# A two-layer diffusion backbone on one core: the recurrence issued in a written order, and the second layer's modulation moved to the first feed-forward

## The chip, the cores and the metric

The kernel runs on one core of a Trainium2 chip. A core has a matrix engine (PE, whose weight loads are listed as PEld), a vector engine (DVE), a scalar engine (ACT) and GpSimd (POOL), each with its own queue that it works off in order, and DMA queues issued from SyncE (SP) and from POOL. The metric is the device time of one execution in microseconds. A difference under 0.3%, some 4.8 us, can't be told from no change by a measurement of this kernel.

## What is computed

Two layers over 256 latent tokens and 256 context tokens of width 1024, all in float32. Each layer is: half-step SwiGLU, token mixing, half-step SwiGLU, each with shift, scale and gate from a conditioning vector. Layer 0 mixes with a bidirectional RWKV-7 recurrence (12 heads of 64, in 6 pairs) and a Fourier mix; layer 1 (latent tokens alone) with a convolution and pooling.

```python
m_lat = split(silu(c) @ ada_w[i] + ada_b[i], 9)          # 9 x 1024 modulation values, layers 0 and 1
h = h + 0.5 * m[2] * swiglu(modulate(h, g, m[0], m[1]), w_gu, w_down)
# layer 0, for both directions d, first the context, then the latent tokens:
w  = exp(-0.6065 * sigmoid(w0[d] + tanh(wd) @ w_up[d]))
a  = sigmoid(a0[d] + ad @ a_up[d]);  kd = k * (1 + (a - 1) * k_a);  b = kk * a
S  = S * w - (S @ kk) b^T + v kd^T ;  y = S @ r           # per token
o  = (groupnorm(y[0] + y[1]) + bonus) * g
```

## The kernel before

**Stages.** The first feed-forward (both streams, 512 columns) fills 46 to 405 us of the trace; then come the input projection of the mixer (to about 546 us), the recurrence (546 to 865 us) with the output projection at its end, two feed-forwards of the latent stream, the convolution mixer and the last feed-forward. All weight matmuls of the feed-forwards are split into three products of rounded parts: `weight` (L190, L191) casts each 512 KB weight tile on ACT and takes the remainder `wlo` on DVE, and PE runs 24 matmuls on it.

**Modulation.** Layer 0's modulation from the third of its nine vectors on is made in the first feed-forward by `ada_job`: a 1 MB DMA on POOL's queue brings 256 rows of the transposed matrix, and DVE multiplies each 128x1024 half with silu(c) and sums along the row (`adaj`, L281), one instruction per 128 outputs and stream, 80 in all. `ffn(..., jobs=2)` runs two steps of these jobs before each weight pair. Layer 1's whole modulation is made in the recurrence by `ada_wide`: 18 blocks, each with 4 DMAs of 512 KB, 8 matmuls (L260, 512 columns each), a copy, 4 transposes (L268) and a small reduce (L269).

**Recurrence.** The tokens are handled in chunks of 64, in three groups of two head pairs. For a group, `features` (twice, one per pair j) builds decays, keys and queries for both directions; `inverse` inverts the 32x32 triangular blocks of all chunks by an elimination of 30 steps of two DVE instructions (L666, L668), between a transpose Y (L657) and two transposes (L673, L678), and then multiplies blocks together (L687, L698) into F. `chain` then goes through 8 steps, one per chunk (4 of context, 4 of latents): PE makes RH from the state XV and the masked products AG (L784), ACT copies RH (L787), PE applies F (L793), ACT and DVE copy UV (L795, L796), PE updates the state with BK (L804), and DVE adds it to the decayed state Xs of POOL (L776, L811). `prep` of the next step makes the pair products pg (L743, L746), AG's upper half (L750), AG's lower half (L755), RR, rs and BK. `rwkv_out` (twice a group) is the output of one pair: group norm, bonus and gate.

**Order.** Outside the recurrence and after the first feed-forward's start, instructions are ordered by a scheduler that takes each engine's ready instruction of highest priority, and priority follows the order in which the program is written. In the recurrence the program alternates: a piece of chain, then `PR[0] = 6` pieces of side work (features and inverse of the next group, then the outputs of the group before), then 4 to 5 pieces of `ada_wide`, whose matmuls stand at a lower priority.

Of the kernel before, what the change touches and what calls it, by code (L numbers as in the profile page):

```python
# [13 lines left out]
P = 128  # L14
D = 1024
# [64 lines left out]
def lay_out(a):  # L80
# [20 lines left out]
    d["adat"] = w[0].T.reshape(9 * KT // 2, 2, P, D)[KT:].transpose(0, 2, 1, 3)  # L101
    d["ada1"] = w[1].reshape(4, 2, P, 18, 512).transpose(3, 0, 2, 1, 4)
# [31 lines left out]
class Net:  # L134
# [113 lines left out]
    def ada_wide(self, b, pool):  # L248

        nc = self.nc  # L250
        ps = self.bank("ada")
        for q in range(4):
            w = self.wp.tile([P, KT, P], F32, tag="wraw", name=self.nm("wraw"), bufs=4)
            w = w.rearrange("p k c -> p (k c)").rearrange("p (k n) -> p k n", k=2)
            nc.sync.dma_start(w, self.ins["ada1"][b, q])
            for i in range(2):
                k = 2 * q + i
                g = k % 4
                with self.tc.high_priority(-200):
                    nc.tensor.matmul(ps[32 * g:32 * g + 32, :], lhsT=self.cs[:, k, :], rhs=w[:, i, :],  # L260
                                     start=k < 4, stop=k >= 4, tile_position=(0, 32 * g), skip_group_check=True)
                if i:
                    yield
        sb = self.mp.tile([P, 512], F32, tag="adas", name=self.nm("adas"), bufs=1)
        nc.scalar.copy(sb, ps)
        pt = self.bank("ada")
        for i in range(4):
            nc.tensor.transpose(pt[:, i * P:(i + 1) * P], sb[:, i * P:(i + 1) * P], self.ident)  # L268
        nc.vector.tensor_reduce(out=self.mod[1, 0][:, 4 * b:4 * b + 4], in_=pt.rearrange("p (b g v) -> p b v g", b=4, g=4)[:, :, 0, :],  # L269
                                axis=AX.X, op=ALU.add)  # L270
        yield

    def ada_job(self, blk, vecs):
# [269 lines left out]
    def features(self, G, j, wa, kz, vz, rz):  # L543
        nc, mp, ins = self.nc, self.mp, self.ins
        c = lambda t: t[:, j:j + 1]
        up = mp.tile([P, 2, P], F32, tag="up", name=self.nm("up"), bufs=1)
# [16 lines left out]
        yield  # L563
# [802 lines left out]
```

## Time and profile before

| | |
|---|---|
| device time, median of 3 runs | 1596.66 us (1593.55 to 1597.36) |
| profiled execution: device time, span of the trace | 1593.66 us, 1592.0 us |
| PE busy in the span, mean granted clock | 1488.8 us (94%), 0.963 |
| DVE, ACT, POOL busy | 1082.7, 675.4, 202.3 us |
| chain that ended last, share of the span | PE 80%, DVE 13% |

Times in the trace are microseconds from the span's start. A window gives each engine's busy time in a stretch, and the share of full speed that PE's clock was granted there (1.00 is 2.4 GHz, 0.50 would be 1.2 GHz throughout).

### The profile page before, as it was taken

What the parts mean: (1) busy time and instruction counts of PE and PEld (TensorE: products, weight loads), DVE (VectorE), ACT (ScalarE), POOL (GpSimd) and SP (SyncE); (2) the same over time, 40 slices, a digit from 0 to 9 for tenths busy, and PEclk for the clock granted to TensorE, in tenths of its full rate; (3) what the DMA queues carried; (4) which work ended last, traced back from release to release, by engine and by line L of the source; (5) the groups of instructions that cost most, each with busy time, mean ns of one, the idle gap of its engine ahead of it and who ended that gap; (6) DMA issues with size and microseconds to landing.
All of it is one profiled execution on the core that took longest, in us unless ns stands there. A gap on an engine that the chain in (4) does not pass through costs nothing.

```text
span 1592.0 us, 29925 instructions
## 1 busy us (share of the span) xinstructions
PE 1488.8 (94%) x12102; PEld 1279.8 (80%) x12102; DVE 1082.7 (68%) x1994; ACT 675.4 (42%) x1101; POOL 202.3 (13%) x293
## 2 busy tenths in 40 slices
PE   5999999999989979899998999999999986899997
PEld 3788888888877755455686999999999874899997
DVE  4799963334689699577266777657775399767753
ACT  3422222223454462542444555445554365445542
POOL 0000100000131151321211000000000075200000
PEclk9999999999999889999799999999999988899999
DMA  9676953232322025455432555655556432345562
GB/s 373 236 238 235 335 200 103 93 92 82 125 84 84 28 102 203 169 197 194 150 108 69 171 181 180 179 190 173 186 176 178 137 106 92 121 161 184 183 181 88
DMA packets 68810, 253.40 MB, mean 159 GB/s; under 512 B 8032, under 2 KB 10864, under 8 KB 63936
## 3 DMA queue, kind: packets, MB, share of 16 engines
q1 hardware_dynamic: 64080, 219.46, 42.0%
q0 software_dynamic: 4592, 32.03, 5.7%
q8 instruction: 95, 1.56, 0.4%
q14 instruction: 43, 0.35, 0.1%
HBM read 249.36 MB, written 2.10 MB: 158 GB/s over the span
## 4 chain that ended last, share of the span: by engine, by line
PE 80%; DVE 13%; ACT 2%; issue 2%; POOL 1%; DMA 1%; SPq 0%; POOLq 0%; DVEq 0%; ACTq 0%
PE gu L195 13%; PE gu L196 13%; PE gu L197 13%; PE down L195 7%; PE down L196 7%; PE down L197 7%; PE ada L260 3%; PE gu L970 1%; PE gu L1055 1%; DVE wlo L191 1%; DVE oo L1028 1%; DVE ocv L1028 1%; PE pg L746 1%; PE down L804 1%; PE misc L631 1%
## 5 line engine op out<-in xcount | busy, mean ns | idle before, releaser
L190 ACT CAST whi<-wraw 128x1024 fp32r<-128x1024 f32 (+1 forms) x298 | 304.6, 1026 | 524.1 <-PE gu L196 227.2
L191 DVE TENSOR_TENSOR wlo<-wraw,whi 128x1024 fp32r<-128x1024 f32 (+1 forms) x298 | 356.3, 1198 | 151.9 <-ACT whi L190 144.9
L195 PE MATMUL gu<-yh,whi 128*128 128x258 f32 (+1 forms) x1408 | 438.3, 312 | 6.2 <-ACT yh L375 4.3
L196 PE MATMUL gu<-yl,whi 128*128 128x258 f32 (+1 forms) x1408 | 437.7, 311 | 0.1
L197 PE MATMUL gu<-yh,wlo 128*128 128x258 f32 (+1 forms) x1408 | 436.8, 310 | 0.0
L195 PEld LDWEIGHTS gu<-yh,whi 128*128 128x128 f32 x1408 | 265.8, 189 | 24.1 <-ACT yh L375 5.7
L196 PEld LDWEIGHTS gu<-yl,whi 128*128 128x128 f32 x1408 | 267.2, 190 | 15.1 <-DVE yl L377 1.0
L197 PEld LDWEIGHTS gu<-yh,wlo 128*128 128x128 f32 x1408 | 267.3, 190 | 14.9 <-DVE wlo L191 0.8
L196 PE MATMUL down<-hl,whi 128*128 128x256 f32 (+1 forms) x704 | 217.3, 309 | 0.0
L195 PE MATMUL down<-hh,whi 128*128 128x256 f32 (+1 forms) x704 | 217.3, 309 | 0.0
L197 PE MATMUL down<-hh,wlo 128*128 128x256 f32 (+1 forms) x704 | 217.3, 309 | 0.0
L196 PEld LDWEIGHTS down<-hl,whi 128*128 128x128 f32 x704 | 134.4, 191 | 7.4
L195 PEld LDWEIGHTS down<-hh,whi 128*128 128x128 f32 x704 | 134.4, 191 | 7.4
L197 PEld LDWEIGHTS down<-hh,wlo 128*128 128x128 f32 x704 | 134.4, 191 | 7.4
L350 POOL TENSOR_TENSOR rs<-ms,mhalf 128x2 f32<-128x2 f32 (+1 forms) x9 | 10.9, 1208 | 821.4 <-DVE ms L347 821.4
L281 DVE SCALAR_TENSOR_TENSOR adaj<-adaw,cb 128x1024 f32<-128x1024 f32 x80 | 97.7, 1221 | 4.9 <-DMA adaw<-in_adat_dram 3.6
L260 PE MATMUL ada<-wraw,ccs 128*32 128x512 f32 x288 | 71.5, 625 | 0.7 <-DVE mod L269 0.7
L384 DVE SCALAR_TENSOR_TENSOR hlat<-down,mc,hlat 128x256 f32<-128x256 f32 x46 | 22.2, 483 | 63.0 <-PE down L197 63.0
L438 DVE COPY wb<-gu 128x1 f32<-128x1 f32 x132 | 20.2, 153 | 46.6 <-PE gu L197 46.6
L360 ACT CAST hh<-hd 128x256 fp32r<-128x256 f32 (+1 forms) x88 | 40.4, 461 | 25.0 <-DVE hd L433 14.2
L970 PE MATMUL gu<-yo,wraw 128*128 128x256 f32 x192 | 45.4, 396 | 1.9 <-ACT yo L375 1.9
L1012 POOL TENSOR_TENSOR opart<-opart,opr 128x256 f32<-128x256 f32 x54 | 44.9, 832 | 5.0 <-ACT opr L1010 1.2
(341 smaller groups left out, 2311.9 us busy)
## 6 DMA issues: line engine op xcount, KB each, us to landing
wraw<-in_gu_dram SPq DMA_DIRECT2D x176, 512.0 KB, 4.0
wraw<-in_ada_dram SPq DMA_DIRECT2D x72, 512.0 KB, 4.3
adaw<-in_adat_dram POOLq DMA_DIRECT2D x28, 1024.0 KB, 5.6
wraw<-in_down_dram SPq DMA_DIRECT2D x64, 448.0 KB, 3.3
wraw<-in_down_dram SPq DMA_DIRECT2D x32, 512.0 KB, 3.5
wraw<-in_win_dram SPq DMA_DIRECT2D x22, 512.0 KB, 3.8
wraw<-in_owin_dram SPq DMA_DIRECT2D x14, 512.0 KB, 3.6
ada<-in_ada_dram SPq DMA_DIRECT2D x4, 1024.0 KB, 16.8
```

The lines of the kernel that those rows point to most:

```text
L190: nc.scalar.copy(hi[:, :k, :], raw[:, :k, :])
L191: (eng or nc.vector).tensor_tensor(out=lo[:, :k, :], in0=raw[:, :k, :], in1=hi[:, :k, :].bitcast(F32), op=ALU.subtract)
L195: mm(ps, lhsT=wh, rhs=xh, start=start, stop=False, **k)
L196: mm(ps, lhsT=wh, rhs=xl, start=False, stop=False, **k)
L197: mm(ps, lhsT=wl, rhs=xh, start=False, stop=stop, **k)
L260: nc.tensor.matmul(ps[32 * g:32 * g + 32, :], lhsT=self.cs[:, k, :], rhs=w[:, i, :], start=k < 4, stop=k >= 4, tile_position=(0, 32 * g), ...
L281: nc.vector.scalar_tensor_tensor(out=junk, in0=w[:, i, :], scalar=1.0, in1=self.cb[v], op0=ALU.mult, op1=ALU.mult, accum_out=self.mod[0, v ...
L360: self.nc.scalar.copy(hi, x)
L384: nc.vector.scalar_tensor_tensor(out=h[v][:, k, :], in0=ps[:, n * T:n * T + T], scalar=gate[v][:, k:k + 1], in1=h[v][:, k, :], op0=ALU.mul ...
L970: nc.tensor.matmul(ps[:, :n], lhsT=w[:, k, :], rhs=y[:, k, :], start=k == 0, stop=k == KT - 1)
L1012: nc.gpsimd.tensor_tensor(out=part, in0=prev, in1=pr, op=ALU.add)
L1028: nc.vector.scalar_tensor_tensor(out=c, in0=u[:, w:w + T], scalar=cw[:, j, w:w + 1], in1=c, op0=ALU.mult, op1=ALU.add)
```

## The change

Three things are changed. `ada_wide` is gone, and 36 more `ada_job`s for layer 1 are appended to the list of the first feed-forward, which now takes three steps of it at each call. The recurrence is written inside a block in which PE, DVE, ACT and POOL keep the program's order: `chain` yields three times a step (after RH, after UV, at the step's end), and after each the class `Beside` lets the side work go on by 2.4, 2.6 or 1.7 us (by group) of costs that are written at the side work's yields. And some instructions change engine: AG's lower half, one half of ar, ac and the `f` of the decay from DVE to POOL; rs from DVE to ACT; the small copies pc and ps from POOL to ACT.

```diff
-    def ada_wide(self, b, pool):
...
-    def ada_job(self, blk, vecs):
+    def ada_job(self, l, blk, vecs):
...
-        nc.gpsimd.dma_start(w, self.ins["adat"][blk // 2 - KT])
+        nc.gpsimd.dma_start(w, self.ins["adat"][l * 9 * KT // 2 + blk // 2 - KT])
...
-                                               op1=ALU.mult, accum_out=self.mod[0, v][:, blk + i:blk + i + 1])
+                                               op1=ALU.mult, accum_out=self.mod[l, v][:, blk + i:blk + i + 1])
...
+            nc.gpsimd.tensor_scalar(out=f[:, :, 1:], in0=c8(th), scalar1=1.0, scalar2=1.0, op0=ALU.add, op1=ALU.mult)
...
-            nc.gpsimd.tensor_copy(G["pc"][:, x, :], em[:, :, CW])
+            nc.scalar.copy(G["pc"][:, x, :], em[:, :, CW])
...
-            nc.vector.tensor_tensor(out=G["ac"][:, x], in0=kr[:, 1], in1=em[:, NCH:, 0:CW], op=ALU.mult)
-            nc.vector.tensor_tensor(out=G["ar"][:, x, :, 1, :], in0=ch(rev(rz))[:, 0], in1=em[:, 0:NCH, 1:], op=ALU.mult)
+            nc.gpsimd.tensor_tensor(out=G["ac"][:, x], in0=kr[:, 1], in1=em[:, NCH:, 0:CW], op=ALU.mult)
+            nc.gpsimd.tensor_tensor(out=G["ar"][:, x, :, 1, :], in0=ch(rev(rz))[:, 0], in1=em[:, 0:NCH, 1:], op=ALU.mult)
...
-                nc.vector.tensor_tensor(out=AG[lo, hd], in0=G["ac"][r, :, c, :] if s else G["ar"][r, :, c, 0, :], in1=pc,
...
+                nc.gpsimd.tensor_tensor(out=AG[lo, hd], in0=G["ac"][r, :, c, :] if s else G["ar"][r, :, c, 0, :], in1=pc,
...
+                nc.scalar.copy(rs[lo], G["ar"][up, :, c, 1, :])
...
+class Beside:
+
+
+    def __init__(self):
+        self.gens, self.left = [], 0.0
+
+    def run(self, us):
+        self.left = min(self.left + us, us)
+        while self.gens and self.left > 0:
+            r = next(self.gens[0], self)
+            if r is self:
+                self.gens.pop(0)
+            else:
+                self.left -= 1.0 if r is None else r
+
+    def rest(self):
+        drive(self.gens, 1000)
...
+                    net.jobs += [net.ada_job(1, k, (0,)) for k in range(0, 9 * KT, 2)]
...
-                    net.ffn(0, h, yh, yl, gate, acc, fp, 2, start)
+                    net.ffn(0, h, yh, yl, gate, acc, fp, 3, start)
...
-            wide = [net.ada_wide(b, lp) for b in range(18)]
             outs = []
+            order = tc.manual_schedule(engines={mybir.EngineType.PE, mybir.EngineType.DVE, mybir.EngineType.Activation,
+                                                mybir.EngineType.Pool})
+            order.__enter__()
...
-                while next(it, it) is not it:
-                    drive(side, PR[0])
-                    drive(wide, PR[1 + g])
-                drive(side, 1000)
+                for _ in it:
+                    side.run((2.4, 2.6, 1.7)[g])
                 outs = [net.rwkv_out(*y, gs) for y in G[g]["y"]]
+                if g < 2:
+                    it = net.chain(G[g + 1], lp)
+                    next(it)
+                side.rest()
+            order.__exit__(None, None, None)
```

The outputs of group 0 join the list of group 1's stage behind its features and inverse, and what the slices don't reach is issued by `rest`, after the next chain's first preparation.

How PE's order moves is seen in chain 0, in one of its later steps. Before, between the matmuls that make RH (L784) and those that apply F (L793), stand matmuls and transposes of `ada_wide` (L260, L268):

```order
L784 MATMUL down_5632<-XV_5284,AG_5546 64x64
L260 MATMUL ada_5241<-wraw_5492,ccs 32x512
L260 MATMUL ada_5241<-wraw_5496,ccs 32x512 x2
L746 MATMUL pg_5681<-ar_3317,bk_3313 128x128 x2
L268 MATMUL ada_5502<-cst,adas_5500 128x128 x4
L732 MATMUL mx_5667<-cst,z_3301 128x128
L732 MATMUL mx_5667<-cst,vr_5669 128x128
L784 MATMUL down_5632<-XV_5284,AG_5546 64x64 x7
L732 MATMUL mx_5667<-cst,z_3481 128x128
L732 MATMUL mx_5667<-cst,vr_5673 128x128
L746 MATMUL pg_5681<-ar_3317,bk_3314 128x128 x2
L793 MATMUL down_5643<-RH_5641,A_3319 64x64 x8
L746 MATMUL pg_5681<-ar_3317,bk_3315 128x128 x2
L746 MATMUL pg_5681<-ar_3317,bk_3316 128x128 x2
```

After, at the like step, RH is L822 and F is L833, and BK's transposes (L749), the pair products (L764) and the state update (L845) follow as written:

```order
L822 MATMUL down_5536<-XV_5187,AG_5423 64x64 x8
L749 MATMUL mx_5550<-cst,bk_3529 128x128
L749 MATMUL mx_5550<-cst,bk_3530 128x128
L749 MATMUL mx_5550<-cst,bk_3531 128x128
L749 MATMUL mx_5550<-cst,bk_3532 128x128
L833 MATMUL down_5569<-RH_5545,A_3535 64x64 x8
L764 MATMUL pg_5580<-ar_3533,bk_3529 128x128 x2
L764 MATMUL pg_5580<-ar_3533,bk_3530 128x128 x2
L764 MATMUL pg_5580<-ar_3533,bk_3531 128x128 x2
L764 MATMUL pg_5580<-ar_3533,bk_3532 128x128 x2
L845 MATMUL down_5596<-UV_5188,BK_5431 64x64 x8
```

The matmuls on `wraw` are gone from between the chain's products, and RH's eight stand in one piece.

On DVE, in the elimination of the same group, before: chain instructions (UV L796, AG L750 and L755, XV L811, RR L759) alternate one by one with elimination instructions:

```order
L666 TENSOR_TENSOR sub_5172<-Y_5151,Z_5152 128x150
L668 TENSOR_TENSOR Z_5152<-Z_5152,sub_5172 128x25x6
L666 TENSOR_TENSOR sub_5175<-Y_5151,Z_5152 128x168
L796 TENSOR_SCALAR UV_5285<-down_5526 64x4x64
L668 TENSOR_TENSOR Z_5152<-Z_5152,sub_5175 128x24x7
L750 TENSOR_TENSOR AG_5546<-pg_5547,cst 64x512
L666 TENSOR_TENSOR sub_5178<-Y_5151,Z_5152 128x184
L755 TENSOR_TENSOR AG_5680<-ar_3317,pc_3320 64x256
L668 TENSOR_TENSOR Z_5152<-Z_5152,sub_5178 128x23x8
L811 TENSOR_TENSOR XV_5284<-down_5537,Xs_5513 64x4x64
L666 TENSOR_TENSOR sub_5181<-Y_5151,Z_5152 128x198
L759 TENSOR_TENSOR RR_5559<-pg_5547,cst 128x512
```

After (elimination L657 and L659, UV L836, AG's upper half L768), eight elimination instructions stand together ahead of UV, and AG's lower half is not on DVE:

```order
L657 TENSOR_TENSOR sub_5560<-Y_5407,Z_5408 128x210
L659 TENSOR_TENSOR Z_5408<-Z_5408,sub_5560 128x21x10
L657 TENSOR_TENSOR sub_5563<-Y_5407,Z_5408 128x220
L659 TENSOR_TENSOR Z_5408<-Z_5408,sub_5563 128x20x11
L657 TENSOR_TENSOR sub_5566<-Y_5407,Z_5408 128x228
L659 TENSOR_TENSOR Z_5408<-Z_5408,sub_5566 128x19x12
L836 TENSOR_SCALAR UV_5188<-down_5569 64x4x64
L768 TENSOR_TENSOR AG_5547<-pg_5580,cst 64x512
L657 TENSOR_TENSOR sub_5590<-Y_5407,Z_5408 128x234
L659 TENSOR_TENSOR Z_5408<-Z_5408,sub_5590 128x18x13
L657 TENSOR_TENSOR sub_5593<-Y_5407,Z_5408 128x238
L659 TENSOR_TENSOR Z_5408<-Z_5408,sub_5593 128x17x14
```

What moved is the elimination, from single instructions in gaps to pieces of eight between the chain's.

On DVE in the first feed-forward, some 36 weight tiles into it, before: the last row sums are done, and the rows are remainders (`wlo`) and the gate's products (hd, hl):

```order
L433 TENSOR_TENSOR hd_1630<-sg_1629,gu_1604 128x512
L191 TENSOR_TENSOR wlo_1790<-wraw_1791,whi_1789 128x1024
L361 TENSOR_TENSOR hl_1338<-hd_1630,hh_1337 128x512
L191 TENSOR_TENSOR wlo_1821<-wraw_1822,whi_1820 128x1024
L433 TENSOR_TENSOR hd_1704<-sg_1703,gu_1678 128x512
L191 TENSOR_TENSOR wlo_1871<-wraw_1872,whi_1870 128x896
L361 TENSOR_TENSOR hl_1338<-hd_1704,hh_1337 128x512
```

After, at a later weight tile (about the 60th of 68), row sums (L255, `adaj`) still stand three to a remainder:

```order
L190 TENSOR_TENSOR wlo_2718<-wraw_2719,whi_2717 128x1024
L335 TENSOR_TENSOR hl_2246<-hd_2550,hh_2245 128x512
L255 SCALAR_TENSOR_TENSOR adaj_2969,mod_77<-adaw_2967,cb 128x1024
L271 SCALAR_TENSOR_TENSOR mc_2442_13965<-mc_2442_13965,smallc 128x8
L255 SCALAR_TENSOR_TENSOR adaj_2971,mod_77<-adaw_2967,cb 128x1024
L255 SCALAR_TENSOR_TENSOR adaj_2975,mod_77<-adaw_2973,cb 128x1024
L190 TENSOR_TENSOR wlo_2749<-wraw_2750,whi_2748 128x1024
L255 SCALAR_TENSOR_TENSOR adaj_3013,mod_77<-adaw_2973,cb 128x1024
```

## Rows read from the trace of the kernel before

**Rows 1.** The page's first part: busy time, share of the span, instructions.

```profile
PE 1488.8 (94%) x12102; PEld 1279.8 (80%) x12102; DVE 1082.7 (68%) x1994; ACT 675.4 (42%) x1101; POOL 202.3 (13%) x293
```

**Rows 2.** Windows: stretch, length, busy PE, PEld, DVE, ACT, POOL (count); clock, DMA share, GB/s.

```profile
546.50:591.80 45.30, 36.55 (x580) 24.98 (x579) 37.89 (x65) 28.98 (x53) 22.64 (x34) 0.89 0.24 86
591.80:639.50 47.70, 45.30 (x580) 27.39 (x580) 44.44 (x115) 15.29 (x37) 7.92 (x11) 1.00 0.53 188
639.50:647.00 7.50, 7.18 (x273) 5.36 (x271) 2.02 (x6) 7.17 (x11) 1.89 (x2) 1.00 0.07 25
647.00:699.50 52.50, 47.38 (x577) 25.25 (x577) 34.50 (x61) 23.79 (x44) 21.68 (x30) 0.90 0.52 178
699.50:754.10 54.60, 50.53 (x572) 27.55 (x570) 43.37 (x112) 16.51 (x37) 7.83 (x12) 1.00 0.57 206
754.10:763.40 9.30, 9.24 (x265) 8.50 (x266) 0.43 (x3) 6.72 (x12) 1.87 (x4) 0.53 0.52 195
763.40:865.00 101.60, 93.83 (x931) 68.81 (x929) 55.69 (x119) 38.75 (x78) 20.20 (x22) 0.91 0.29 95
```

**Rows 3.** Windows of line L260 alone, over the recurrence; the sum.

```profile
sum 319.00, PE 71.50 PEld 10.56; mean PE 23.83 PEld 3.52
```

**Rows 4.** The chain of waits by line, 546 to 865 us.

```profile
by line: PE ada L260 15.2%; PE pg L746 5.4%; PE down L804 5.1%; PE misc L631 4.1%; issue 3.9%; PE down L784 3.8%; PE down L793 3.6%; DVE ff L591 3.3%; PE ada L268 2.8%; PE mx L765 2.7%; PE mx L829 2.3%; PE mx L823 2.2%; DVE AG L750 1.7%; PE
```

**Rows 5.** Groups of lines on DVE, 593 to 636 us (count; busy, mean ns; idle before).

```profile
L668 DVE TENSOR_TENSOR Z<-Z,sub 128x30 f32<-128x30 f32 (+14 forms) x30 | 10.9, 365 | 0.5
L666 DVE TENSOR_TENSOR sub<-Y,Z 128x30 f32<-128x30 f32 (+14 forms) x30 | 10.8, 359 | 0.5
L750 DVE TENSOR_TENSOR AG<-pg,cst 64x512 f32<-64x512 f32 x6 | 4.2, 695 | 0.4 <-PE pg L743 0.2
L755 DVE TENSOR_TENSOR AG<-ar,pc 64x256 f32<-64x256 f32 x6 | 3.4, 572 | 0.1
L811 DVE TENSOR_TENSOR XV<-down,Xs 64x256 f32<-64x256 f32 x8 | 3.4, 420 | 0.6 <-PE down L804 0.4
L796 DVE TENSOR_SCALAR UV<-down 64x256 f32<-64x256 f32 x5 | 2.1, 425 | 0.3 <-ACT UV L795 0.2
L673 DVE STREAM_TRANSPOSE A<-Z 128x1024 f32<-128x1024 f32 x1 | 2.0, 1995 | 0.0
```

**Rows 6.** Timeline of ACT: start, length, two successive copies of RH.

```profile
844.46 0.41 ACT L787 COPY RH<-down 128x256 f32<-128x256 f32 x1
851.08 0.37 ACT L787 COPY RH<-down 128x256 f32<-128x256 f32 x1 [5.04 <-PE down L784]
```

**Rows 7.** The page's costliest groups: the row sums of the first feed-forward.

```profile
L281 DVE SCALAR_TENSOR_TENSOR adaj<-adaw,cb 128x1024 f32<-128x1024 f32 x80 | 97.7, 1221 | 4.9 <-DMA adaw<-in_adat_dram 3.6
```

**Rows 8.** Windows of the first feed-forward.

```profile
160.00:200.00 40.00, 40.00 (x176) 32.64 (x175) 37.25 (x61) 9.83 (x12) 5.51 (x11) 1.00 0.93 337
220.00:400.00 180.00, 180.00 (x810) 147.97 (x809) 68.32 (x96) 48.52 (x67) 0.00 (x0) 1.00 0.30 95
```

**Rows 9.** Timelines of POOL and DVE around 599 us.

```profile
599.19 1.05 POOL L776 TENSOR_TENSOR Xs<-XV,pcs 64x512 f32<-64x512 f32 x1 [2.83 <-DVE XV L811]
599.29 1.05 DVE L668 TENSOR_TENSOR Z<-Z,sub 128x84 f32<-128x84 f32 x1
```

**Rows 10.** Timeline of DVE: first and last DVE work of one output (j).

```profile
763.56 0.42 DVE L849 SCALAR_TENSOR_TENSOR f<-misc,yy 128x256 f32<-128x256 f32 x1 [8.99 <-PE misc L847]
773.22 0.42 DVE L873 TENSOR_TENSOR z<-f,misc 128x256 f32<-128x256 f32 x1 [0.90 <-POOL f L870]
```

**Rows 11.** Windows of 20 us: one in the recurrence, one in the odd mixer.

```profile
760.00:780.00 20.00, 18.65 (x190) 11.56 (x184) 5.24 (x15) 8.64 (x17) 3.00 (x3) 0.67 0.32 116
1320.00:1340.00 20.00, 8.22 (x32) 6.41 (x31) 20.00 (x39) 10.51 (x24) 9.16 (x12) 0.79 0.18 60
```

**Rows 12.** Timeline of PE: a group of 16 in a slow stretch, one in a fast.

```profile
763.88 1.12 PE L784 MATMUL down<-XV,AG 64*64 64x64 f32 x16
851.51 0.68 PE L793 MATMUL down<-RH,A 64*64 64x64 f32 x16 [0.52 <-ACT RH L787]
```

More of the change, by code (lines that the diff above doesn't have):

```diff
@@ L558, in features @@
             nc.tensor.matmul(pt[:, 2 * i:2 * i + 2], lhsT=sq[:, P * i:P * i + P], rhs=self.hsel, start=True, stop=True)
+        for u, hi, lo in halves:
+            nc.vector.tensor_tensor(out=u[lo], in0=up[hi], in1=u[hi].bitcast(F32), op=ALU.subtract)
         mx = mp.tile([P, 4, 2], F32, tag="mx", name=self.nm("mx"), bufs=2)
@@ new lines, in values @@
+        def values(step):
+            s, c, _ = at(step)
+            ps = self.bank("ada")
+            for x in range(4):
+                v = G["v"][x][:, s, :]
+                if x % 2:
+                    vr = t([P, P], "vr", 2)
+                    nc.gpsimd.tensor_copy(vr, v[:, ::-1][:, c * CW:c * CW + P])
+                else:
+                    vr = v[:, c * CW:c * CW + P]
+                nc.tensor.transpose(ps[:, x * P:x * P + P], vr, self.ident)
+            for q in range(2):
+                V[step + q] = [t([P, 4, 2, CW], tag, 3) for tag in ("XV", "UV")]
+                for w in V[step + q]:
+                    nc.scalar.copy(w[up], xhi(ps)[CW * q:CW * q + CW])
@@ new lines, in keys @@
+        def keys(step, S):
+            s, c, ch = at(step)
+            S["XV"], S["UV"] = V.pop(step)
+            AG = S["AG"] = t([P, 2, 4, CW], "AG", 2)
+            for hd in range(2 if step else 0):
+                r = slice(CW * hd, CW * hd + CW)
+                pc = G["pc"][r, :, at(step - 1)[2]].unsqueeze(2).to_broadcast([CW, 4, CW])
+                nc.gpsimd.tensor_tensor(out=AG[lo, hd], in0=G["ac"][r, :, c, :] if s else G["ar"][r, :, c, 0, :], in1=pc,
+                                        op=ALU.mult)
+            if step < 7:
@@ L762, in prep, with outputs @@
-            if step < 7:
-                ps = self.bank("mx")
-                for x in range(4):
-                    nc.tensor.transpose(ps[:, x * P:x * P + P], G["bk"][x][:, ch, :], self.ident)
-                BK = S["BK"] = t([P, 4, P], "BK", 2)
-                nc.scalar.copy(BK.rearrange("p x j -> p (x j)"), ps)
-        S = {}
-        prep(0, S)
+                nc.scalar.copy(rs[lo], G["ar"][up, :, c, 1, :])
+        def outputs(step, S, Xs):
+            s, c, ch = at(step)
+            ps = self.bank("mx")
+            p3 = half(ps)
+            UV = S["UV"]
+            rv = lambda x, t: t[:, ::-1] if x % 2 else t
+            for x in range(4):
+                for hd in range(2):
+                    o = CW * hd
+                    mm(p3[o:o + CW, x, :], lhsT=UV[:, x, hd, :], rhs=rv(x, S["RR"][:, hd, x, :]),
+                       start=x == 0, stop=False, tile_position=(0, o), skip_group_check=True)
+            for x in range(4):
+                for hd in range(2):
+                    o = CW * hd
+                    r = S["rs"][lo, x, :] if hd else G["ar"][lo, x, c, 1, :]
+                    mm(p3[o:o + CW, x, :], lhsT=Xs[lo, x, hd, :], rhs=rv(x, r),
+                       start=False, stop=True, tile_position=(0, o), skip_group_check=True)
+            for x in range(4):
+                y = Y[x // 2][:, 3 - c if x % 2 else c, :]
+                if c < 2:
+                    nc.scalar.copy(y, p3[:, x, :])
+                else:
+                    nc.vector.tensor_tensor(out=y, in0=p3[:, x, :], in1=y, op=ALU.add)
@@ L787, in chain @@
             nc.scalar.copy(RH, p3)
-            ps = self.bank("down")
-            p3 = ps[:, :T].rearrange("p (x i) -> p x i", x=4)
+            if step < 7:
+                keys(step + 1, N)
+            yield
+            p3 = half(self.bank("down"))
             for x in range(4):
@@ L1230, in body @@
             net.mp = mp
[L1231 removed]
+            z, G, first = {}, {}, Beside()
             for i, m in enumerate(order):
```

241 lines of the change are left out of this document (103 added, 138 removed).

## The prediction

> **What bounds the kernel now.** I read the page first: PE is busy 94% of the span [rows 1], so a gain must come from a stretch in which PE either waits or does work that can go elsewhere. The recurrence is that stretch. The windows cut it at what its side work does [rows 2]: features of group 1 with their block products (45.3 us, to the transpose Y), elimination with the transposes at its ends (47.7), block products of the tail (7.5), the same three for group 2 (52.5, 54.6, 9.3), and the third chain with outputs and projection (101.6); 318.5 us in all. PE looks full in each, but 71.5 us of it are the wide modulation matmuls alone [rows 3], and the chain of waits runs through them for 15.2% of 319 us and through their transposes for 2.8% [rows 4], 57 us. What else bounds differs by window: in the features DVE is busy 37.9 of 45.3 us with ACT at 29.0 and POOL at 22.6, nobody full; in the elimination DVE is busy 44.4 of 47.7, and the elimination's own 60 instructions there idle 1.0 us before them [rows 5], so DVE is its bound. A chain step alone needs little: the two closest copies of RH lie 6.6 us apart [rows 6], so 8 steps want 53 us where the stages take 101, 116 and 102.
>
> **Row sums in the first feed-forward.** Added are 72 row sums of 1.22 us and as many accumulator reads (the mean of 80 [rows 7]), with the read and the gap to the next an estimated 1.26 each, 91 us of DVE, and 36 DMAs of 1 MB. From 220 to 400 us PE is busy 180.0 of 180.0, DVE only 68.3, DMA at 0.30 [rows 8]. With 91 added DVE stands at 159 of 180. It does more than that at 160 to 200 us, 37.25 of 40, with DMA at 0.93, and PE is still at 40.00 of 40 [rows 8]; the order shows three row sums to a remainder, the same pace, now until about the 60th of 68 weights. So I price this at 0. The cover is the remainders' lead over PE; if it is gone each late remainder stalls PE, and I bound that by 8 us (eight weights at the end without a lead, 1 us each). Below nothing: no reason for a gain there.
>
> **What the recurrence loses.** 144 matmuls, 72 transposes, 18 copies and 18 reduces, and 72 DMAs on SP's queue ahead of the weights of the projection. Were nothing in their place, 57 us would come off; that is the far bound of the gain. But those 57 us were partly filler while PE waited for others anyway, so I price the windows one by one.
>
> **Features.** The sum of DVE, ACT and POOL work is 89.5 us in the first window and 80.0 in the second, overlapped 1.98-fold and 1.52-fold [rows 2]; in the second the wide matmuls take more of PE. After, a fourth chain step lies in this stretch (+4 us over the three engines), POOL is slower at what it takes over (+3), the copies of the wide blocks go (-2): about 95. At the better overlap this is 48 us, at the worse 62. The order of four engines is now fixed, so nobody can pass a waiting instruction: against it stands that PE no longer delays anyone. I take 48: +2.7 and -4.5. Below, the busiest engine would be ACT or POOL with some 34 us each (29.0 and 22.6 plus what moves there), which is the floor.
>
> **Elimination.** Its own instructions take 21.7 us, and three chain steps instead of nearly five lie beside them, each with AG's upper half .70, XV .84, UV .43 and, by my estimate, .8 for RR and the outputs: 2.75 each, 8.2 in all. Three transposes of 2.0 make 6 [rows 5]. Between Y and the first step a negation on ACT and a mask on POOL have to pass, an estimated 4 us. That is 40; AG's lower half (3.4 us for six) leaves DVE. But POOL collides: the Xs that starts at 599.19 and lasts 1.05 stretches the elimination instruction beside it to 1.05 [rows 9] where the mean is .37 [rows 5], .7 us lost. AG's lower half adds two POOL instructions a step of half that size; 3 steps at .7 make 2, and I take 42 for each group: -5.7 and -12.6. Bounds: 36 (no collision, the 4 us hidden) and 50.
>
> The Trainium skill (SBUF — State Buffer, section on the two separate sides) says that DVE and GpSimd share a port pair as an exclusive lock, and that a DVE instruction with two SBUF inputs is fully blocked by a GpSimd one that reads SBUF. The trace agrees: the two end within 0.1 us of each other [rows 9]. By that rule all six lower halves in an elimination (an estimate of .53 each, half of 1.05) would hold DVE, 3.2 us instead of 2, and my sum would be some 2 us higher.
>
> **Tail and third stage.** The tail goes from 7.5 and 9.3 to 8 each (at 9.3 the clock stood at 0.53): +0.5 and -1.3. In the third stage the outputs of group 0 now stand in front, with only the chain's first preparation beside them, one after the other. One took 9.7 us from its first DVE instruction to its last with wide matmuls between [rows 10]; I take 14 for two. Then 8 steps at 9.7 (6.6 plus the DVE and PE share of outputs, Fourier and projection), 78, and 3 to the end: 95 against 101.6, -6.6. Bounds 75 and 104.
>
> **Clock.** PE without filler idles more. At 760 to 780 us the granted clock is 0.67, and at 1320 to 1340, with PE busy 8.2 of 20, 0.79 [rows 11]. Over the seven windows it is 0.93 by length [rows 2]. If it falls to 0.8, a quarter more of the time is at 1.2 GHz; a chain step has three groups of 16 matmuls on its path, and one took .68 where the clock was full, 1.12 where it was not [rows 12], some .4 more each; so 1.2 x 16 steps (in the eliminations DVE hides it) x 0.25 = +5.
>
> The Trainium skill (TensorE: Matmul & The Clock Gate, part on the clock gate) says that a gate sets the clock by how busy PE has been recently; the trace agrees at 1320 to 1340 us, where PE idles more than half the time and the clock is below full [rows 11]. Were the low level granted throughout the recurrence, 24 steps at 1.2 would cost 29 us.
>
> **Sum.** 2.7 - 4.5 - 5.7 - 12.6 + 0.5 - 1.3 - 6.6 = -27.5; with the clock -22.5; the mixer's input projection, where the same moves from DVE to POOL act on group 0, I leave at 0 (3 either way). The profiled execution took 1593.7, so 1571; it lies 3.0 under the median of the runs shown, which makes 1574.
>
> **Rivals.**
> *All of the filler's chain time comes off.* For it: 57 us in the chain of waits [rows 4]. Against: without it DVE, ACT and POOL are the next to wait for, and the fixed order binds them. 1597 - 57 = 1540.
> *No change.* Half the overlap is lost: features at 55 (+10, +2.5), elimination at 46 (-1.7, -8.6), third stage as before: +2 and the clock's 5, against some gain in the tail; 1594 to 1602. For it: DVE was the bound of the elimination and stays so.
> *Slower: the fixed order makes the features run one behind the other.* Place: the two features stretches, where an ACT copy that waits for PE holds back the tanh behind it, that the POOL multiply, that the scan. Price: at the second window's overlap of 1.52, 62 us each, +14 more in each than I take, so +28 on 1574: 1602; at 1.4, 68 each, 1614. It decides from 59 us each on. For it: in the second window of before all three engines are under 66% busy. Against: there the wide matmuls stood in between.
>
> **Chances.** Forecast (1555 to 1588) 0.45, all of it (1535 to 1554) 0.15, no change 0.14, slower 0.26. Faster than by 0.3% (4.8 us) is 0.60, within it 0.14, slower 0.26. The range leaves out a tenth at each side: low by the full gain, 1541; high in the slower rival, 1606.
>
> **What would show it.** First feed-forward: PE busy 180 of 180 at 220 to 400 us with DVE near 159, and its last update not more than 8 us later. Features windows: 48 us, DVE below 33, POOL above 30. Elimination with transposes: 42 us, DVE above 85% busy. Third stage 95 us, the two outputs 14 of it. Mean granted clock in the recurrence near 0.8. I am wrong if the features stretch exceeds 59 us, if remainders come late in the first feed-forward, or if DVE idles in the elimination behind chain instructions that wait for PE.

## The result: slower by 3.1%

The changed kernel takes 1646.27 us (median of 4 runs, 1643.07 to 1651.12), the kernel before 1597.01 in the same session (4 runs): a ratio of 1.031, 95% interval 1.028 to 1.035. That is outside the range given, 1541 to 1606, and on the other side of no change: the likeliest case was 1574. Of the rivals, the one that ends slower names the mechanism, but neither all of its places nor its size.

On the changed kernel's page, the line that answers to [rows 1]: PE works 29 us less, the span is 54 us longer (1646.3).

```profile
PE 1459.7 (89%) x11742; PEld 1304.6 (79%) x11742; DVE 1132.8 (69%) x2030; ACT 676.2 (41%) x1131; POOL 264.5 (16%) x371
```

The windows that answer to [rows 2], cut at the ends of the same work of each stage; the first begins 2.6 us ahead of the first copy of RH (L825, at 561.36), as the first of [rows 2] does (its copy is at 549.12). Columns are as there.

```profile
558.70:623.50 64.80, 41.86 (x637) 32.66 (x636) 32.32 (x49) 32.52 (x68) 34.05 (x41) 0.68 0.02 5
623.50:663.90 40.40, 24.37 (x348) 20.65 (x348) 36.49 (x83) 11.43 (x28) 10.44 (x16) 0.72 0.01 1
663.90:675.30 11.40, 11.40 (x304) 10.59 (x301) 1.34 (x6) 7.38 (x14) 2.44 (x5) 0.50 0.01 3
675.30:735.40 60.10, 37.40 (x584) 29.34 (x582) 29.46 (x44) 29.40 (x63) 33.56 (x39) 0.66 0.01 4
735.40:778.30 42.90, 26.66 (x316) 22.62 (x316) 38.95 (x85) 10.83 (x27) 9.55 (x14) 0.63 0.00 1
778.30:789.80 11.50, 11.44 (x306) 10.17 (x306) 1.04 (x5) 5.68 (x11) 2.31 (x3) 0.50 0.32 101
789.80:920.30 130.50, 99.55 (x940) 79.67 (x940) 49.31 (x101) 40.06 (x83) 28.73 (x41) 0.76 0.14 44
```

Against 45.3, 47.7, 7.5, 52.5, 54.6, 9.3 and 101.6 before, the features take 64.8 and 60.1 us, the eliminations 40.4 and 42.9, the tails 11.4 and 11.5, the third stage 130.5: 361.6 in all for 318.5, 43.1 more. The stretch itself begins 12.2 us later (558.7 for 546.5): 7.0 us in the first feed-forward, as the next rows show, and 5.2 between it and the recurrence. The latter need not be the change's: e4 below, the same program up to there, takes 144.2 us from the feed-forward's last matmul to the first copy of RH, the kernel before 144.4, the changed kernel 149.7. 43.1 and 12.2 make the 54.3 us by which the span grew, within 1 us. Of the 361.6 us PE is busy 252.7 and DVE 188.9: outside the eliminations and the tails no engine is full, and the engines wait. The mean clock of PE there is 0.69, and in the tails 0.50, which is 1.2 GHz throughout.

In the first feed-forward, windows that answer to [rows 8]:

```profile
160.00:200.00 40.00, 40.00 (x176) 32.64 (x175) 37.41 (x64) 9.50 (x11) 5.81 (x11) 1.00 0.95 358
220.00:400.00 180.00, 176.28 (x760) 143.38 (x759) 146.24 (x241) 46.95 (x63) 16.90 (x32) 0.99 0.77 286
```

PE, which had idled nowhere in these 180 us, now stands 3.7 us, and the feed-forward's last matmul starts 7.0 us later (411.67 for 404.70). These 3.7 us lie between 240 and 260 us. The waits at 236 to 264 us show the longest piece (engine, line, what it waited for: us in total, times, longest):

```profile
ACT hh L334 <- DVE hd L407: 13.5, 2, 7.5
PE down L194 <- ACT hh L334: 3.3, 1, 3.3
```

The matmuls of the down projection wait for `hh`, ACT's cast, which waits for `hd` on DVE, and DVE has row sums ahead of it: the last matmul that `hd` needs is done by 250.5, and `hd` starts at 256.51, behind four row sums and a remainder.

```profile
256.51 0.68 DVE L407 TENSOR_TENSOR hd<-sg,gu 128x512 f32<-128x512 f32 x1
257.89 0.50 PE L194 MATMUL down<-hh,whi 128*128 128x512 f32 x1 [3.27 <-ACT hh L334]
```

What the waits in the recurrence look like is seen first in the features of group 1, in the first chain's first step. Its copy of RH is done at 561.73, but F (L833) stands behind matmuls of the features, which wait for ACT and POOL, and starts at 572.22. Further on a transpose of `vr` for the next step (L729) waits 7.69 us for POOL, and the next RH, whose XV is ready at 578.61, stands behind it and starts at 584.10:

```profile
564.31 1.87 PE L540 MATMUL misc<-cst,f 128*128 128x2 f32 x8 [2.15 <-ACT f L536]
568.24 1.98 PE L619 MATMUL misc<-cst,inv 128*64 128x128 f32 x16 [2.06 <-POOL ff L561]
572.22 0.70 PE L833 MATMUL down<-RH,A 64*64 64x64 f32 x10
...
583.27 0.47 PE L729 MATMUL ada<-cst,vr 128*128 128x128 f32 x1 [7.69 <-POOL vr L726]
```

On POOL the copy `vr` stands behind the features' `ff`, which waits 3.86 us for ACT, and behind ac and ar:

```profile
579.13 1.16 POOL L562 TENSOR_SCALAR ff<-f 128x512 f32<-128x512 f32 x1 [3.86 <-ACT f L557]
...
582.46 0.75 POOL L726 COPY vr<-z 128x128 f32<-128x128 f32 x1
```

This step takes 25.0 us from copy to copy of RH. Another is in the third chain: ACT's copies of RH (L825) stand 17.1 us apart, where [rows 6] show 6.6.

```profile
849.90 0.37 ACT L825 COPY RH<-down 128x256 f32<-128x256 f32 x1 [3.33 <-PE down L822]
...
866.97 0.37 ACT L825 COPY RH<-down 128x256 f32<-128x256 f32 x1 [10.73 <-PE down L822]
```

Between them DVE works on a projection tile (`wo` L335, the remainder of its weight) and the chain's XV (L850) and RR (L774) in one queue:

```profile
855.24 1.23 DVE L335 TENSOR_TENSOR wo<-wraw,wo 128x1024 fp32r<-128x1024 f32 x1
858.73 0.48 DVE L358 SCALAR_TENSOR_TENSOR hY<-misc,mc,hY 128x256 f32<-128x256 f32 x1 [2.26 <-PE misc L196]
859.42 0.85 DVE L850 TENSOR_TENSOR XV<-down,Xs 64x256 f32<-64x256 f32 x2 [0.21 <-PE down L845]
860.31 0.69 DVE L774 TENSOR_TENSOR RR<-pg,cst 128x512 f32<-128x512 f32 x1
860.91 1.64 DVE L335 TENSOR_TENSOR wo<-wraw,wo 128x1024 fp32r<-128x1024 f32 x1
```

and PE on the projection (L194 to L196) and the chain's state update (L845) and RH (L822) in one queue:

```profile
856.52 0.39 PE L196 MATMUL misc<-oh,wo 128*128 128x256 f32 x1 [1.23 <-DVE wo L335]
...
858.62 0.69 PE L845 MATMUL down<-UV,BK 128*64 128x64 f32 x16
...
859.46 0.28 PE L195 MATMUL misc<-ol,wo 128*128 128x256 f32 x1
862.61 0.43 PE L196 MATMUL misc<-oh,wo 128*128 128x256 f32 x1 [2.87 <-DVE wo L335]
...
865.83 0.41 PE L196 MATMUL misc<-oh,wo 128*128 128x256 f32 x1
866.17 0.69 PE L822 MATMUL down<-XV,AG 128*64 128x64 f32 x16
```

UV is whole at 854.26, but BK's update stands behind eighteen projection matmuls of which the third waits 1.23 us for `wo`: it starts at 858.62. XV is ready at 860.27; the next RH starts at 866.17, behind another piece of projection that waited 2.87 us for a `wo` which DVE had to make after XV and RR. So the chain waits in PE's queue behind the projection, the projection waits for DVE, and in DVE's queue its `wo` stands behind the chain.

### The profile page after: what moved, and what is told of

Its sections match the earlier page's. It is cut to its first block, busy times and chain, and to the rows that moved or that the text cites. A ratio compares the mean times of both kernels' runs of the same rounds, so it can differ in the third digit from the quotient of the medians.

```text
span 1646.3 us, 29235 instructions
## 1 busy us (share of the span) xinstructions
PE 1459.7 (89%) x11742; PEld 1304.6 (79%) x11742; DVE 1132.8 (69%) x2030; ACT 676.2 (41%) x1131; POOL 264.5 (16%) x371
## 3 DMA queue, kind: packets, MB, share of 16 engines
q0 software_dynamic: 9776, 69.78, 11.4%
## 4 chain that ended last, share of the span: by engine, by line
PE 47%; DVE 10%; ACT 3%; POOL 2%; issue 2%; POOLq 0%; DVEq 0%; ACTq 0%
PE gu L194 8%; PE gu L196 8%; PE gu L195 8%; PE down L196 4%; PE down L195 4%; PE down L194 4%; PE gu L992 1%; DVE sub L657 1%; PE gu L1077 1%; DVE Z L659 1%; DVE oo L1050 1%; DVE ocv L1050 1%; PE misc L619 1%; DVE wo L335 1%; PE down L833 1%
## 5 line engine op out<-in xcount | busy, mean ns | idle before, releaser
L194 PE MATMUL gu<-yh,whi 128*128 128x258 f32 (+1 forms) x1408 | 438.9, 312 | 6.2 <-ACT yh L349 4.3
L196 PE MATMUL gu<-yh,wlo 128*128 128x258 f32 (+1 forms) x1408 | 437.2, 311 | 0.0
L194 PEld LDWEIGHTS gu<-yh,whi 128*128 128x128 f32 x1408 | 266.1, 189 | 24.1 <-ACT yh L349 5.6
L196 PEld LDWEIGHTS gu<-yh,wlo 128*128 128x128 f32 x1408 | 267.8, 190 | 14.7 <-DVE wlo L190 0.5
L194 PE MATMUL down<-hh,whi 128*128 128x256 f32 (+1 forms) x704 | 217.9, 310 | 3.3 <-ACT hh L334 3.3
L196 PE MATMUL down<-hh,wlo 128*128 128x256 f32 (+1 forms) x704 | 217.8, 309 | 0.0
L255 DVE SCALAR_TENSOR_TENSOR adaj<-adaw,cb 128x1024 f32<-128x1024 f32 x152 | 185.6, 1221 | 10.4 <-DMA adaw<-in_adat_dram 8.9
L194 PEld LDWEIGHTS down<-hh,whi 128*128 128x128 f32 x704 | 134.7, 191 | 11.3 <-ACT hh L334 4.0
L196 PEld LDWEIGHTS down<-hh,wlo 128*128 128x128 f32 x704 | 134.9, 192 | 7.4
L251 POOL DMA_DIRECT2D adaw<-in_adat_dram x64 | 33.9, 529 | 284.8 <-DVE adaj L255 189.5
L334 ACT CAST hh<-hd 128x256 fp32r<-128x256 f32 (+1 forms) x88 | 40.4, 460 | 58.4 <-DVE hd L407 47.4
L992 PEld LDWEIGHTS gu<-yo,wraw 128*128 128x128 f32 x192 | 39.8, 208 | 8.5 <-ACT yo L349 2.1
```

What stands on the lines that cost most here:

```text
L194: mm(ps, lhsT=wh, rhs=xh, start=start, stop=False, **k)
L196: mm(ps, lhsT=wl, rhs=xh, start=False, stop=stop, **k)
L251: nc.gpsimd.dma_start(w, self.ins["adat"][l * 9 * KT // 2 + blk // 2 - KT])
L334: self.nc.scalar.copy(hi, x)
L992: nc.tensor.matmul(ps[:, :n], lhsT=w[:, k, :], rhs=y[:, k, :], start=k == 0, stop=k == KT - 1)
```

## The experiments

Three theories. **Series**: with the order of all engines fixed, a slice of side work, whose instructions depend on each other across engines, stands in series with the chain's slice. **Clock**: without the wide matmuls PE falls to the lower level, and that is the loss. **POOL**: the work moved there is slower and collides with DVE. All ratios are to the kernel before, measured in the same session. Where a length of the recurrence is given for a run, it goes from the first copy of RH to the first matmul of the next feed-forward, in the one profiled execution: 326.6 us in the kernel before (549.12 to 875.73), 369.7 in the changed kernel (561.36 to 931.05).

### e1: the scheduler orders the recurrence

```diff
-            order = tc.manual_schedule(engines={mybir.EngineType.PE, mybir.EngineType.DVE, mybir.EngineType.Activation,
-                                                mybir.EngineType.Pool})
-            order.__enter__()
...
-            order.__exit__(None, None, None)
```

> The changed kernel without the block that fixes the order: the scheduler again takes what is ready in the recurrence; everything else of the change stays, so PE still has no filler and POOL the moved work. If the fixed order makes the engines wait behind each other (theory order), the 374 us of the recurrence after (551 to 925) fall back to some 300 or less, and the time to 1575 or less. If the missing filler's clock is the cause (theory clock), PE is as slow as in the changed kernel (granted clock 0.5 to 0.8 there) and the time stays over 1620. If the work moved to POOL is the cause, likewise.

1590.17 us, ratio 0.994 (0.992 to 0.996). The fixed order alone costs 56 us by the medians, 60 in the recurrence. The recurrence of the changed kernel, then that of e1:

```profile
561.36:931.05 369.69, 260.69 (x3424) 212.04 (x3425) 196.19 (x386) 141.31 (x301) 121.06 (x156) 0.70 0.08 26
558.84:868.49 309.65, 237.75 (x3412) 190.37 (x3413) 199.50 (x382) 139.52 (x296) 128.63 (x152) 0.78 0.09 31
```

309.7 us at a clock of 0.78, where the changed kernel takes 369.7 at 0.70. PE's work is the same but for a few records, and takes 22.9 us longer in the changed kernel; a slower clock can explain at most these 22.9 of the 60.0 us, and the other 37 are waits. So the clock isn't the main part of what makes the changed kernel slow. The time is not the 1575 that the series theory had put as a bound: the first RH comes 9.7 us later than before, and the scheduler's own order gains less from the missing matmuls than I had thought (e2).

### e2: only the row sums moved

The kernel before with `ada_wide` and its calls taken out, the jobs of both layers in the list and `net.ffn(..., 3, start)`.

> The kernel before with one part of the change: the wide modulation matmuls are gone and the 72 row sums stand in the first feed-forward; order and engines of the recurrence as before. Theory order: the 57 us that the wide matmuls held in the chain of waits come off in good part, 1550 to 1580, less the 4 us stall seen at 240 to 260 us of the changed kernel. Theory clock: the recurrence's clock falls under 0.8 and it is no faster than before, 1590 to 1640.

1593.10, ratio 0.996 (0.994 to 0.997): a gain of 0.4%, far from the 1550 to 1580 of the theory order and inside the 1590 to 1640 of the theory clock. The recurrence takes 318.6 us where it took 326.6, at a clock of 0.76 for 0.93: the 57 us of wide matmuls in the chain of waits were worth 8 us net. PE is busy 253.4 us of it; before it was 295.8, of which 70.5 and 13.4 were the wide matmuls and their transposes, so that the other work takes an estimated 41 us longer. Here the clock can have eaten most of the gain; how much of these 41 us lies on the path that ends last, no run shows.

### e3: the moved work back on DVE

```diff
-            nc.gpsimd.tensor_scalar(out=f[:, :, 1:], in0=c8(th), scalar1=1.0, scalar2=1.0, op0=ALU.add, op1=ALU.mult)
+            nc.vector.tensor_scalar(out=f[:, :, 1:], in0=c8(th), scalar1=1.0, scalar2=1.0, op0=ALU.add, op1=ALU.mult)
```

and so for ac, the half of ar and AG's lower half.

> The changed kernel with f, ac, the half of ar and AG's lower half back on DVE, in the same fixed order. If POOL's longer instructions and its collisions with DVE are the cause, 1620 or less; if order or clock is, within 10 us of 1646 either way.

1642.50, ratio 1.026 (1.024 to 1.028), against 1.031. The recurrence takes 370.9 us, for 369.7: the work moved to POOL is not the cause of what it loses.

### e4: filler in the fixed order

```diff
-                for _ in it:
+                for i, _ in enumerate(it):
+                    if i % 3 < 2:
+                        ps = net.bank("ada")
+                        for _ in range(2):
+                            nc.tensor.matmul(ps, lhsT=net.ident, rhs=net.cst[:, 0:512], start=True, stop=True)
                     side.run((2.4, 2.6, 1.7)[g])
```

> The changed kernel with two matmuls of 512 columns on constants, results unread, after the first and the second slice of each chain step, 96 in all, some 60 us of PE at full clock. Theory clock: the granted clock in the recurrence rises from about 0.68 to over 0.85 and the time falls by 15 us or more, to 1630 or less. Theory order: the clock rises, but the time stays within 10 us of 1646 or grows by the filler that stands in the way, up to 1690.

1662.52, ratio 1.039 (1.035 to 1.042). The clock did rise, to 0.88 in the recurrence, and the stretch got 14 us longer:

```profile
555.77:939.76 383.99, 309.25 (x3616) 207.08 (x3617) 196.08 (x386) 141.61 (x301) 121.02 (x156) 0.88 0.08 25
```

The filler brings the higher clock and 49 us more of busy PE together; what the clock would give by itself this run does not show.

### e5: chain and side work one after the other

```diff
                 for _ in it:
-                    side.run((2.4, 2.6, 1.7)[g])
+                    pass
                 outs = [net.rwkv_out(*y, gs) for y in G[g]["y"]]
+                side.rest()
                 if g < 2:
                     it = net.chain(G[g + 1], lp)
                     next(it)
-                side.rest()
```

> The changed kernel, still in the fixed order, but no side work between the chain's slices: each chain runs alone, then its group's side work alone. Theory series (in the fixed order a slice of side work, whose instructions depend on each other across engines, stands in series with the chain's slice, so that little overlaps): no more than 30 us above the changed kernel, 1646 to 1675. If the interleaving does overlap the two and the loss lies elsewhere (clock, POOL), the 24 chain steps at 6.6 us or more come on top, less what the slices lose: over 1720.

1650.71, ratio 1.032 (1.029 to 1.035), against 1.031: no clear difference from the changed kernel. The windows are chain alone, side alone, three times:

```profile
559.00:600.00 41.00, 33.01 (x621) 27.57 (x618) 17.45 (x37) 19.29 (x49) 15.60 (x23) 0.96 0.01 2
600.00:684.00 84.00, 32.43 (x643) 26.64 (x639) 53.34 (x98) 30.11 (x56) 31.00 (x36) 0.57 0.02 4
684.00:726.00 42.00, 34.22 (x613) 28.51 (x612) 17.46 (x37) 18.70 (x49) 15.59 (x23) 0.93 0.01 2
726.00:823.00 97.00, 40.00 (x676) 30.78 (x672) 57.13 (x109) 31.75 (x60) 34.44 (x40) 0.60 0.06 21
823.00:863.00 40.00, 32.14 (x619) 26.46 (x615) 17.46 (x37) 18.29 (x47) 15.58 (x23) 1.00 0.01 2
863.00:928.00 65.00, 43.98 (x260) 34.50 (x259) 25.70 (x52) 17.61 (x28) 6.96 (x8) 0.89 0.24 77
```

The chains alone take 41, 42 and 40 us (some 5 us a step), the side work 84, 97 and 65. The recurrence takes 377.9 us apart and 369.7 interleaved: of some 120 us of chain the written interleaving saves 8. From one chain's first RH to the next it saves 11 and 7 us (113.9 for 124.6, 131.8 for 139.2), and in the third stage it loses 10 (123.9 for 114.1). The clock differs too: the chains alone run at 0.93 to 1.00, and PE's work takes 222.8 us here for 260.7 interleaved. So it is shown that the written interleaving gains next to nothing; how much overlap there is that the lower clock takes back is not.

### e6: filler where the order is free

e1 with the matmuls of e4 under `tc.high_priority(-200)`, as `ada_wide` had them.

> The changed kernel without the fixed order, as in the first run (1590), and with 96 matmuls of 512 columns on constants at lower priority than the rest, results unread. Theory clock as the second loss: the recurrence's clock rises from 0.77 to about 0.9 and the time falls by 5 us or more, to 1585 or less. If the clock costs nothing there because DVE, ACT and POOL are waited for, the time stays at 1590 or grows by up to 30.

1616.12, ratio 1.011 (1.008 to 1.013): 26 us slower than e1, at a clock of 0.95 in the recurrence for 0.78.

```profile
560.30:896.13 335.83, 300.43 (x3604) 197.01 (x3605) 198.60 (x384) 138.44 (x298) 128.06 (x152) 0.95 0.09 29
```

PE is busy 63 us more than in e1 for 26 us of time (335.8 for 309.7). So this filler costs more by standing in the way than its clock gives back, at a lower priority too; the 8 us that e2 gained by taking the wide matmuls out fit that.

### e7: the third chain's order free

```diff
                 else:
+                    order.__exit__(None, None, None)
                     gate = net.modcol(0, 0, 5)
```

> The changed kernel with the fixed order ended before the third chain, which the scheduler orders. Theory series: the third stage, 135 us in the changed kernel where it was 102 before, falls to about 90, and the time to about 1605. If the third stage is slow for its clock (0.76), it stays over 120 us and the time over 1635.

1614.07, ratio 1.008 (1.005 to 1.011), 32 us under the changed kernel. The last RH of the second chain and the first matmul of the next feed-forward:

```profile
782.91 0.37 ACT L825 COPY RH<-down 128x256 f32<-128x256 f32 x1
...
```

```profile
895.67 0.72 PE L194 MATMUL gu<-yh,whi 128*128 128x258 f32 x4 [0.67 <-ACT yh L1350]
```

113 us, where the changed kernel takes 152 (778.64 to 931.05) and the kernel before 135. These 40 us off the changed kernel's 130.5 make the 90 that the series theory expected for the third stage; the time stays 9 us over its 1605.

### e8: the row sums in mixed order, order free

e1, and the jobs with two streams are put among those with one:

```diff
+                    both, one = net.jobs[5:13], net.jobs[13:]
+                    net.jobs = net.jobs[:5]
+                    for i, job in enumerate(one):
+                        if both and i % 6 == 0:
+                            net.jobs.append(both.pop(0))
+                        net.jobs.append(job)
```

> The changed kernel without the fixed order, and with the row sums of two streams mixed among those of one, so that the DMA does not stand at 0.97 from 160 to 340 us. If the 3 to 4 us that PE stalls at 240 to 260 us come from row sums on DVE that wait for their DMA, they go: PE busy 180 of 180 at 220 to 400 us, and the time 3 to 4 us under the first run's 1590. If DVE's load itself is the cause, no change.

1583.06, ratio 0.990 (0.988 to 0.993): 1% under the kernel before, and 7 us under e1 by the medians, though the intervals of the two ratios overlap.

```profile
220.00:400.00 180.00, 178.46 (x787) 145.54 (x786) 148.94 (x247) 48.55 (x66) 15.34 (x29) 1.00 0.73 263
```

PE idles 1.5 us instead of 3.1 in e1, and the feed-forward's last matmul starts at 407.98, not 409.75. DVE has no less to do and the DMA share is 0.73 where the changed kernel had 0.77, so the pace of the loads may have been part of the stall, not all. These 2 us are less than the 7 between e1 and e8. The recurrence is no shorter (311.1 us for 309.7): the rest lies in the projection of the mixer between the two, which takes 144.2 us in e4 and 149.7 in e5, the same program up to there; so it can't be put down to the jobs' order.

### e9 and e12: parts of e8

e9 is e2 with the mixed jobs. e12 is e8 with the edits of e3.

> The kernel before with the row sums in the first feed-forward in mixed order and without the wide matmuls; order and engines of the recurrence as before. Beside e8 (1583, the same with the change's slices and moves under the scheduler). If only the jobs' order matters, 1586 to 1590, 4 to 7 below the 1593 of the unmixed one; if the slices and moves matter under the scheduler too, it stays some 4 above e8.

> The scheduler-ordered version with mixed row sums (e8, 1583), with f, ac, the half of ar and AG's lower half back on DVE. If the moves to POOL help when the order is free, 3 us or more slower than e8; if they cost as much by collisions as they free, within 3 us of 1583; if collisions cost more, 1580 or less.

e9: 1591.98, ratio 0.996 (0.994 to 0.998), no better than e2's 0.996, and 9 us above e8 where some 4 had been expected. e12: 1582.54, ratio 0.990 (0.988 to 0.992), the same as e8. With a free order the four moves to POOL are worth nothing either way. What sets e8 and e12 apart from e9, some 0.6%, is the rest of the change: the slices of chain and side work, which set the scheduler's priorities, and the copies rs, pc and ps moved to ACT. No run separates these two.

### e10, e11, e13, e14, e15: which queue

The changed kernel with the order fixed on some engines alone, by the set handed to `manual_schedule`.

> The changed kernel with only PE's order fixed; DVE, ACT and POOL are ordered by the scheduler. If PE's queue is the one in which dependent work stands in series (side matmuls that wait for ACT or DVE ahead of the chain's), most of the 56 us remain, 1630 to 1646. If DVE, ACT or POOL are, 1590 to 1605.

> The changed kernel with the order of DVE, ACT and POOL fixed, PE's left to the scheduler. If PE's queue is the cause, 1590 to 1610; if any of the other three is enough by itself to put the two in series, 1625 to 1646.

> The changed kernel with only DVE's order fixed. If DVE's queue is the one that puts chain and side in series (chain instructions wait behind side ones that wait for ACT, POOL or PE), 1610 or more, near the 1624 of the three together; if not, 1588 to 1600.

> The changed kernel with only ACT's order fixed. ACT makes the copies of RH, half of UV and BK on the chain's path and stood waiting for PE ahead of them most often in the changed kernel (RH 23 us and UV 14 us in the third stage). If its queue is the cause, 1610 or more; if not, 1588 to 1600.

> The changed kernel with only POOL's order fixed. POOL has the powers (1.66 us) and the moved products; Xs waited there for 64 us in the third stage, but waiting on an engine with little to do need not delay anyone. If POOL's queue is the cause, 1610 or more; if not, 1588 to 1600. If all three single runs stay under 1600, it takes several fixed queues together.

| order fixed on | median us | ratio, interval | recurrence us |
|---|---|---|---|
| none (e1) | 1590.17 | 0.994 (0.992 to 0.996) | 309.7 |
| POOL (e15) | 1588.00 | 0.993 (0.992 to 0.995) | 310.5 |
| PE (e10) | 1592.67 | 0.997 (0.995 to 0.999) | 316.3 |
| DVE (e13) | 1599.62 | 1.000 (0.998 to 1.002) | 318.9 |
| ACT (e14) | 1605.97 | 1.004 (1.002 to 1.005) | 330.0 |
| DVE, ACT, POOL (e11) | 1623.83 | 1.018 (1.013 to 1.023) | 344.7 |
| all four (changed) | 1646.27 | 1.031 (1.028 to 1.035) | 369.7 |

No single queue carries the loss. Over e1, ACT alone costs 1.0% and DVE 0.6%; PE's 0.3% isn't clear of the intervals, and POOL costs nothing. The singles make 1.9% together, where all four fixed cost 3.7%. The recurrence's length in one execution of each says the same: over e1 20 us for ACT, 9 for DVE, 7 for PE and 1 for POOL, 37 together, where all four cost 60. Two runs lie between the bounds that had been set: ACT alone at 1606, for 1610 or more as the cause, and the three together at 1624, for 1625 or more. So the fixed queues add more than the sum of what each adds alone. A queue that may reorder can take up the waits of one that may not; that this is the reason is argued, not shown.

## Why the prediction was wrong

- **Row sums at 0.** The mechanism was the bounded one, and the size was off: the feed-forward ended 7.0 us later, inside the 8 I had as bound. The cover was thought to be the lead of the remainders; what came late was `hd`, in the same DVE queue. That 160 to 200 us could stand this load before did not show that a longer stretch can: PE stood still at 240 to 260 us.
- **57 us in the chain of waits.** Right not to take them: taking them out of the kernel before gains 8 us of the recurrence (e2), and the new slices and moves with them 17 (e1: 309.7 for 326.6). Of the rest the lower clock can take back up to an estimated 41 us in e2; how much it does, and how much DVE, ACT and POOL would have made anyway, the runs do not separate.
- **Features: "at the better overlap this is 48 us".** This is one of the two steps that failed. The three engines' work came out near what I had, 98.9 and 92.4 us in the windows where I had 95, but it overlaps 1.53-fold and 1.54-fold, in 64.8 and 60.1 us: +19.5 and +7.6 instead of +2.7 and -4.5. I took the better of two overlaps that a scheduler had reached, which lets an instruction pass a waiting one, for an order in which none may; the worse, 1.52 and 62 us, was on record beside it. In the second window 95 was luck in part: its 80.0 with the +4, +3 and -2 make 85.
- **Elimination at 42.** Right: 40.4 and 42.9, with DVE busy 36.5 and 39.0, 90% and 91%. Here DVE has nearly all the work, and the fixed order cost nothing.
- **Tails at 8.** 11.4 and 11.5, with PE busy 11.4 at a clock of 0.50: the clock term belonged here, where PE is busy throughout, and the two miss by 7 us.
- **Third stage at 95: "8 steps at 9.7".** The other step that failed, by 35 us. I put a chain step's bare time and a share of engines' work side by side; the steps took 14.0 us each from copy to copy of RH (807.11 to 905.22). In e5, one after the other, the chain alone takes 40 us and the side work alone 65, and from the first RH to the next feed-forward 114.1 us; interleaved it is 123.9, with steps like the one at 850 to 867 us. PE's work is 97.0 us there for 83.2 in e5, so a lower clock may explain that difference, but not the rest. With the order free from there on, 113 us take the place of 152 (e7). The two outputs in front I had at 14; they took 16.7 (789.80 to 806.47).
- **Clock at 0.8, +5.** It fell further, to 0.69. Raised by filler it brought nothing net (e4, e6); what the low clock costs by itself is bounded, at 22.9 us between the changed kernel and e1, and not shown.
- **The sum.** The profiled execution missed its 1571 by 76.8 us: 28.9 in the features, 35.5 in the third stage, 6.9 in the tails, -0.7 in the eliminations, 12.2 ahead of the recurrence, less the 5 that had been added for the clock, which leaves the account within 1 us.
- **The rival on the slower side** was right that the work would run one behind the other. Its 62 us for each of the features met what they took, 64.8 and 60.1, but it left out the third stage, which is worse; its 1602 to 1614 is therefore short of 1646. The sum of the rival of no change was off: its +2 and the clock's 5 on 1597 make 1604, not 1594 to 1602.
- **POOL's collisions** do not decide: with all four moves undone the recurrence takes 370.9 us for 369.7 in the fixed order (e3), and 309.3 for 311.1 in the free one (e12 beside e8). They are there. A lower half of AG takes 0.62 us on POOL (the median of 42), where I had estimated .53. At 861 us of the changed kernel one takes 1.60, beside the `wo` of DVE that runs from 860.91 to 862.55, 1.64 us for its usual 1.23; and that `wo` began while POOL's Xs ran, until 861.47:

```profile
860.42 1.05 POOL L815 TENSOR_TENSOR Xs<-XV,pcs 64x512 f32<-64x512 f32 x1 [14.77 <-DVE XV L850]
861.43 1.60 POOL L744 TENSOR_TENSOR AG<-ar,pc 64x256 f32<-64x256 f32 x1
```

  The Trainium skill (SBUF — State Buffer, section on the two separate sides) says that DVE and GpSimd share a port pair as an exclusive lock: whichever of two such instructions starts first gets it for the whole instruction, and the other fully blocks. The trace agrees in both directions: Xs came first and `wo` took 0.41 us longer, `wo` came first and AG took 0.98 us longer and ended 0.48 us after it.

## What to carry to other kernels

An order written by hand on all engines fixes every queue, and two chains of dependent work that alternate in such queues can nearly add up, as here, where instructions stand in a queue before their operands are there. Run the two apart once: if the sum is near the time of the interleaved version, the interleaving gains little, and the clock of both runs tells whether the comparison is even. Price a fixed order by the overlap that it has to rebuild, not by busy sums at the overlap a scheduler reached. Work moved into the idle time of an engine should be tested over the whole stretch that it will fill, and in the queue of whatever it stands ahead of.

## What was not expected of the hardware

A low clock lengthens PE's own work much (by an estimated 41 us in e2, at 0.76 for 0.93), and whole tails ran at 0.50; yet some 17 points of granted clock bought no time in either order (0.70 to 0.88 in e4, 0.78 to 0.95 in e6), where they were paid for with 49 and 63 us more of busy PE.
